# Seven-product pairs of a gated MLP: order of the products, buffers and loads of the weight sums

## Chip, cores and metric

The kernel runs on one core of a Trainium2 chip. The metric is device time in microseconds (us) of one execution, as the median of several runs. The engines are TensorE (PE in the profile, PEld for its weight loads), VectorE (DVE), ScalarE (ACT), GpSimd (POOL) and SyncE (SP, whose queue issues most loads).

## The reference

One decoder layer on 512 tokens of width 1024, in float32. What matters here is its second half, the gated MLP behind the first LayerNorm, with `D_FF` = 2816:

```python
a, u = jnp.split(h @ w_ffn_in[l], 2, axis=-1)
a = causal_dwconv(a, conv_w[l], conv_b[l])        # width 3, along the tokens
f = (jax.nn.gelu(a, approximate=False) * u) @ w_ffn_out[l]
h = layer_norm(ALPHA * h + f, ln2_g[l], ln2_b[l])
```

Ahead of it lie an input projection, block-sparse attention, a pooling branch, two branch projections with gates, an output projection and the first LayerNorm.

## The kernel before

All matrices are float32, and TensorE multiplies them as three products of rounded halves. `split` (L65) makes the halves: ScalarE copies the source into a `hi` tile of the rounded type (L69), and VectorE writes `lo = src - hi` (L70). `mm3` (L182) then issues hi x hi, hi x lo and lo x hi into one accumulator (L184, L185, L186). TensorE's work stands almost without a gap, and everything else is laid out beside it.

Weights come as chunks of 128 x 1024, in the order of a list (`chunks`, L80 to L94). `weights(i)` (L177) makes sure that chunks up to `i + LEAD` (3 ahead) have been fetched; `fetch` (L98) loads a chunk into a `wraw` buffer (three of them) by SP's queue and splits it into a `whi` and a `wlo` buffer from a ring of five (`RING`).

The input projection of the MLP has 22 pairs `f`, each with 128 columns of `a` and 128 of `u`. Pairs 0 to 3 and 18 to 21 are multiplied plainly, 512 tokens at a time. Pairs 4 to 17 (`SEVEN`) use a scheme with seven half-size products in the place of eight: the 2 x 2 blocks are the two halves of the inner dimension (`k1`, `k2`), the two halves of the tokens (`t1`, `t2`), and the weights of `a` and `u`. For it, sums of weights are needed. A pair's four chunks are

- A: the weights of `a`;
- X: the `u` weights' second half added to both halves of `a` (in a rearranged order), made by two DMAs into an `xraw` buffer, a load by SP (L131) and an accumulating one by GpSimd's queue (L132);
- D: the second half of `u`'s weights alone;
- Y: a sum made by VectorE from A and X in two steps (L144).

`fetch_sums` (L126) starts X's two DMAs up to `AHEAD` (5) chunks ahead; `fetch_seven` (L135) loads A and D when their chunk is fetched, forms Y, and splits all four. A, D and Y take `wraw` buffers.

`seven(f)` (L693) does the products of a pair, each of 12 matmuls of 256 columns (`s_mm`, L684), in three PSUM banks: `ba` (its right half is `chain`, in the profile `sa`), `bb` (`low`, `sb`) and `bc` (`c11`, `sc`). Written order: A's first half into `chain` (called A0 below); a ScalarE copy of `chain` into `y` (L699); X0 into `low`; a copy of `low` into `u` (L701); then the left-over product of the pair before (`pending`, Y1 into that pair's `chain`, followed by its `gated`); Y0 onto `chain`; a copy of it into `u` (L705); A1 into `c11`; D0 onto `low`; VectorE adds `low` to `u` (L708); X1 onto `chain`; VectorE adds `chain` to `u` (L710) and writes `y + c11` into the left half of `ba` (L711). Y1 is left for the next pair. `gated` (L621) applies the convolution, gelu and the product with `u`, and writes the pair's slice of `fT`.

The order in the program is a priority, not the order of execution: the instructions of each engine are put into a fixed sequence when the kernel is built, and one may be placed ahead of another that was written earlier if its inputs are planned to be ready sooner. On the chip each engine follows its sequence. Behind the stage the output projection runs on `fT` with sums of its own, and then the second LayerNorm.

Of the kernel before, what the change touches and what calls it, by code (L numbers as in the profile page):

```python
# [8 lines left out]
F32 = mybir.dt.float32  # L9
F32R = mybir.dt.float32r  # L10
AF = mybir.ActivationFunctionType
ALU = mybir.AluOpType
PSUM = bass.MemoryType.PSUM

P = 128
S = 512
D = 1024
# [20 lines left out]
KH = NF // 2  # L38
TAIL = 8
SEVEN = tuple(range(4, 18))  # L40
AHEAD = 5
PRODUCTS = ("T3", "B11", "B21", "T1", "T2", "B22", "T4")


# [1 line left out]
def layer_kernel(ctx: ExitStack, tc: tile.TileContext, xT, x, w_v, w_c, rel_bias, invcnt, w_group,  # L46
                 pscale, w_br, w_out, lnr, w_fi, convp, w_fo, out):
    nc = tc.nc
    const = ctx.enter_context(tc.tile_pool(name="const", bufs=1))
    wp = ctx.enter_context(tc.tile_pool(name="wp", bufs=1))  # L50
# [7 lines left out]
    def bank(name):  # L58
        return ps.tile([P, S], F32, tag="ps", name=name)
# [5 lines left out]
    def split(hi, lo, src, copy=None):  # L65
        if copy:
            copy(hi, src)
        else:
            nc.scalar.activation(hi, src, AF.Copy)  # L69
        nc.vector.tensor_tensor(lo, src, hi.bitcast(F32), op=ALU.subtract)  # L70
# [17 lines left out]
    fi_at = {}  # L88
# [9 lines left out]
    def fetch(pool=None, early=None):  # L98
        i = state["next"]
        state["next"] = i + 1  # L100
        while sums and xu and fi_at[sums[0], "X"] <= i + AHEAD:
            fetch_sums(sums.pop(0))
        if isinstance(chunks[i], tuple):
            ready[i] = (fetch_fo if i >= FO0 else fetch_seven)(i, *chunks[i])
            return
        raw = wp.tile([P, D], F32, tag="wraw", name=f"wraw{i}", bufs=3)
        if pool is None:
            hi = wp.tile([P, D], F32R, tag="whi", name=f"whi{i}", bufs=RING)
            lo = wp.tile([P, D], F32R, tag="wlo", name=f"wlo{i}", bufs=RING)
        else:  # L110
            hi = pool.tile([P, D], F32R, name=f"whi{i}")
            lo = pool.tile([P, D], F32R, name=f"wlo{i}")
        parts = 2 if early else 1
        for c in range(parts):
            sl = slice(c * (D // parts), (c + 1) * (D // parts))
            (nc.scalar if early else nc.sync).dma_start(raw[:, sl], chunks[i][:, sl])
            split(hi[:, sl], lo[:, sl], raw[:, sl], fast if early and c == 0 else None)
            if c == 0 and early:
                early()
        ready[i] = (hi, lo)  # L120

    raws = {}
    sums = list(SEVEN)
    xu = None

    def fetch_sums(f):  # L126
        x_ = raws[f, "X"] = xu.tile([P, D], F32, tag="xraw", name=f"xraw{f}", bufs=2)
        a, u = w_fi[2 * f], w_fi[2 * f + 1]
        v = x_.rearrange("p (a c) -> p a c", a=2)
        (pst, pn), (est, _) = u.ap  # L130
        nc.sync.dma_start(v, bass.AP(tensor=u.tensor, offset=u.offset, ap=[[pst, pn], [0, 2], [est, S]]))  # L131
        nc.gpsimd.dma_start(v, bass.AP(tensor=a.tensor, offset=a.offset,  # L132
                                       ap=[[pst, pn], [u.offset + S - a.offset, 2], [est, S]]), accum_op=ALU.add)

    def fetch_seven(i, f, q):  # L135
        n = S if q == "D" else D
        if q == "X":
            raw = raws[f, "X"]
        else:
            raw = raws[f, q] = wp.tile([P, D], F32, tag="wraw", name=f"wraw{i}", bufs=3)[:, :n]  # L140
        if q == "Y":
            a, x_ = raws[f, "A"], raws[f, "X"]
            for c, o in ((slice(0, S), x_[:, S:]), (slice(S, D), raw[:, :S])):
                nc.vector.tensor_tensor(raw[:, c], o, a[:, c], op=ALU.add)  # L144
        elif q != "X":
            nc.sync.dma_start(raw, w_fi[2 * f] if q == "A" else w_fi[2 * f + 1][:, S:])
        hi = wp.tile([P, D], F32R, tag="whi", name=f"whi{i}", bufs=RING)[:, :n]
        lo = wp.tile([P, D], F32R, tag="wlo", name=f"wlo{i}", bufs=RING)[:, :n]
        split(hi, lo, raw)
        return hi, lo  # L150
# [4 lines left out]
    def piece(c):  # L155
        return slice(c * D, min((c + 1) * D, KH * S))
# [20 lines left out]
    def weights(i):  # L177
        while state["next"] <= min(i + LEAD, state["limit"]):
            fetch()
        return ready[i]  # L180

    def mm3(out_, w, a, start, stop, **kw):  # L182
        (wh, wl), (ah, al) = w, a
        nc.tensor.matmul(out_, wh, ah, start=start, stop=False, **kw)  # L184
        nc.tensor.matmul(out_, wh, al, start=False, stop=False, **kw)  # L185
        nc.tensor.matmul(out_, wl, ah, start=False, stop=stop, **kw)  # L186

    def split3(v, a):
        return tuple(t.rearrange("p (a c) -> p a c", a=a) for t in v)
# [30 lines left out]
    for kt in range(KT):  # L220
        xr = aw.tile([P, S], F32, tag="tmp", name=f"xr{kt}", bufs=TMP)
        if kt == 0:
            load_x(kt, xr, slice(0, 256), nc.vector.tensor_copy)
            fetch(early=lambda: load_x(kt, xr, slice(256, 512), nc.vector.tensor_copy))
        else:
            load_x(kt, xr)
            if kt % 2 == 0:
                fetch()
# [271 lines left out]
    ytiles = [ypool.tile([P, S], F32, name=f"y{j}") for j in range(2)]  # L500
# [120 lines left out]
    def gated(j, a, u, sign=None):  # L621
        y = ytiles[j % 2]
        nc.scalar.activation(y, a, AF.Identity, bias=cvp[:, j, 3:4], scale=cvp[:, j, 2:3])
        nc.vector.scalar_tensor_tensor(y[:, 1:], a[:, :S - 1], cvp[:, j, 1:2], y[:, 1:], op0=ALU.mult, op1=ALU.add)  # L624
        nc.vector.scalar_tensor_tensor(y[:, 2:], a[:, :S - 2], cvp[:, j, 0:1], y[:, 2:], op0=ALU.mult, op1=ALU.add)
        nc.scalar.activation(y, y, AF.Gelu)
        if sign:
            nc.vector.scalar_tensor_tensor(fT[:, j, :], y, sign, u, op0=ALU.mult, op1=ALU.mult)
        else:
            nc.vector.tensor_tensor(fT[:, j, :], y, u, op=ALU.mult)  # L630
# [12 lines left out]
    fT = fw.tile([P, NF, S], F32, name="fT")  # L643
# [7 lines left out]
    t1, t2 = slice(0, 256), slice(256, 512)  # L651
    k1, k2 = slice(0, 4), slice(4, 8)
# [26 lines left out]
    for n in ("nT1", "T3", "nT2", "T4"):  # L679
        t_form(n)  # L680
    state["limit"] = len(chunks) - 1
    pending = []

    def s_mm(f, q, part, act_, b, start, skip=True):  # L684
        wh, wl = split3(weights(fi_at[f, q]), 4 if q == "D" else KT)
        for k in range(4):
            mm3(b, (wh[:, 4 * part + k, :], wl[:, 4 * part + k, :]), (act_[0][:, k, :], act_[1][:, k, :]),
                start and k == 0, k == 3, skip_group_check=not start)

    def whole(k, t):  # L690
        return hT_hi[:, k, t], hT_lo[:, k, t]

    def seven(f):  # L693
        ba, bb, bc = (bank(f"s{q}{f}") for q in "abc")
        chain, low, c11 = ba[:, 256:], bb[:, :256], bc[:, :256]
        y = ytiles[f % 2]
        u = xu.tile([P, S], F32, tag="u", name=f"u{f}", bufs=2)
        s_mm(f, "A", 0, whole(k1, t1), chain, True)
        nc.scalar.activation(y[:, t1], chain, AF.Copy)  # L699
        s_mm(f, "X", 0, tt["T3"], low, True)  # L700
        nc.scalar.activation(u[:, t2], low, AF.Copy)  # L701
        if pending:
            pending.pop()()
        s_mm(f, "Y", 0, tt["nT2"], chain, False)
        nc.scalar.activation(u[:, t1], chain, AF.Copy)  # L705
        s_mm(f, "A", 1, whole(k2, t1), c11, True)
        s_mm(f, "D", 0, tt["T4"], low, False)
        nc.vector.tensor_tensor(u[:, t1], u[:, t1], low, op=ALU.add)  # L708
        s_mm(f, "X", 1, tt["nT1"], chain, False)
        nc.vector.tensor_tensor(u[:, t2], u[:, t2], chain, op=ALU.add)  # L710
        nc.vector.tensor_tensor(ba[:, t1], y[:, t1], c11, op=ALU.add)  # L711

        def close():
            s_mm(f, "Y", 1, whole(k2, t2), chain, False)
            gated(f, ba, u, -1.0)

        pending.append(close)
# [3 lines left out]
    xu = xus.enter_context(tc.tile_pool(name="xu", bufs=1, reuse_waits="tile"))  # L721
    last = max(SEVEN)
    for f in range(RING // 2, last + 1):
        if f in SEVEN:
            seven(f)
            continue
        for j in range(max(RING, 2 * f), 2 * f + 2):
            hb[j] = bank(f"fi{j}")
            fi_mm(j, hb[j], slice(0, S))
            if pending:  # L730
                pending.pop()()
        gated(f, hb[2 * f], hb[2 * f + 1])

    spread = []
    for f in range(last + 1, NF):
        for j in range(2 * f, 2 * f + 2):
# [13 lines left out]
            elif pieces:  # L750
                c = piece(pieces.pop(0))
# [3 lines left out]
        if early:  # L755
            c = early.pop(0)
# [176 lines left out]
```

## Time and profile before

| | |
|---|---|
| median of 3 runs | 651.52 us (651.47 to 652.38) |
| profiled execution | 649.74 us, of which the span is 648.0 us |
| granted TensorE clock, mean | 0.996 |
| TensorE busy | 635.7 us (98% of the span) |
| VectorE, ScalarE, GpSimd busy | 449.5, 328.0, 111.6 us |
| matmuls `sa` of the seven-product pairs | first at 348.0, last at 499.4 us |

Busy shares are means over the whole span, and matmuls overlap each other, so a busy TensorE is not one at its peak. Whether TensorE lost time is read from the starts of its matmuls: in an undisturbed stretch those of 256 columns start 0.12 us apart. A row of the timeline has the start, the duration, the engine, the line, the operation and its tiles, and in brackets the idle time before it with what ended it.

### The profile page before, as it was taken

The numbers are of one execution on the slowest core, as the hardware profiler recorded it, in microseconds if no ns is written. First come the engines' busy times: TensorE is split into PE (matmuls) and PEld (weight loads), VectorE is DVE, ScalarE is ACT, GpSimd is POOL, SyncE is SP. The second block draws the span as 40 slices with busy tenths as digits, with TensorE's granted clock in tenths as the row PEclk, the third lists the DMA queues.
The fourth block names the chain that finished last, engine by engine and source line by source line (L and its number), as shares of the span: only waits on it lengthen the run. The fifth ranks groups of instructions, "written<-read, shape, count | busy, mean of one in ns | idle before, by whom it ended". The sixth has DMA issues, their size and how long they took to land.

```text
span 648.0 us, 9322 instructions
## 1 busy us (share of the span) xinstructions
PE 635.7 (98%) x3586; PEld 551.4 (85%) x3586; DVE 449.5 (69%) x666; ACT 328.0 (51%) x475; POOL 111.6 (17%) x153
## 2 busy tenths in 40 slices
PE   9999999999999999999999999999999999999994
PEld 6888787877888888888999999998998888888884
DVE  6466665564532576299667888787986859698596
ACT  6547556675522333215444556455665337465452
POOL 1605361211000123300010101010100201123302
PEclk9999999999999999999999999999999999999998
DMA  9643222212222227404056686677635895989905
GB/s 323 197 166 99 82 81 82 74 67 89 74 95 98 91 98 286 136 1 162 2 150 173 170 208 155 179 179 188 165 128 163 274 264 137 218 188 193 282 4 129
DMA packets 32540, 94.79 MB, mean 146 GB/s; under 512 B 3688, under 2 KB 3944, under 8 KB 32240
## 3 DMA queue, kind: packets, MB, share of 16 engines
q1 hardware_dynamic: 22832, 66.91, 30.4%
q0 software_dynamic: 9088, 26.24, 20.7%
q10 hardware_dynamic: 576, 1.05, 0.5%
q8 instruction: 28, 0.46, 0.3%
q14 instruction: 16, 0.13, 0.1%
HBM read 91.02 MB, written 3.17 MB: 145 GB/s over the span
## 4 chain that ended last, share of the span: by engine, by line
PE 91%; DVE 3%; POOL 2%; DMA 1%; ACT 1%; issue 1%; DVEq 0%; ACTq 0%; POOLq 0%
PE fi L186 5%; PE fi L184 5%; PE fi L185 5%; PE g L184 5%; PE g L186 4%; PE g L185 4%; PE sa L184 4%; PE sa L186 4%; PE sa L185 4%; PE v L285 3%; PE wo L186 2%; PE br L186 2%; PE br L184 2%; PE wo L184 2%; PE wo L185 2%; PE br L185 2%
## 5 line engine op out<-in xcount | busy, mean ns | idle before, releaser
L70 DVE TENSOR_TENSOR wlo<-wraw,whi 128x1024 fp32r<-128x1024 f32 (+1 forms) x119 | 144.1, 1214 | 59.2 <-ACT whi L69 57.7
L69 ACT ACTIVATE whi<-wraw 128x1024 fp32r<-128x1024 f32 (+1 forms) x118 | 117.2, 996 | 131.9 <-PE g L185 23.6
L186 PE MATMUL fi<-hT_hi,wlo 128*128 128x512 f32 (+1 forms) x168 | 56.7, 339 | 0.0
L185 PE MATMUL fi<-hT_lo,whi 128*128 128x512 f32 (+1 forms) x168 | 56.7, 339 | 0.0
L184 PE MATMUL fi<-hT_hi,whi 128*128 128x512 f32 (+1 forms) x168 | 56.4, 340 | 0.0
L184 PE MATMUL g<-xT_hi,whi 128*128 128x512 f32 x128 | 50.3, 393 | 0.0
L186 PE MATMUL g<-xT_hi,wlo 128*128 128x512 f32 x128 | 49.9, 390 | 0.0
L185 PE MATMUL g<-xT_lo,whi 128*128 128x512 f32 x128 | 49.8, 389 | 0.0
L132 POOL DMA_DIRECT2D xraw<-in_w_fi x14 | 17.0, 1215 | 183.7 <-DVE y L624 70.2
L69 ACT ACTIVATE whi<-tw 128x1024 fp32r<-128x1024 f32 (+1 forms) x30 | 29.4, 982 | 21.6 <-DMA tw<-in_w_fo 8.1
L70 DVE TENSOR_TENSOR wlo<-tw,whi 128x1024 fp32r<-128x1024 f32 (+1 forms) x30 | 33.3, 1127 | 8.4 <-ACT whi L69 8.4
L185 PEld LDWEIGHTS fi<-hT_lo,whi 128*128 128x128 f32 x168 | 31.9, 190 | 3.5
L186 PEld LDWEIGHTS fi<-hT_hi,wlo 128*128 128x128 f32 x168 | 31.9, 190 | 3.3
L184 PEld LDWEIGHTS fi<-hT_hi,whi 128*128 128x128 f32 x168 | 31.6, 190 | 3.3
L184 PE MATMUL sa<-hT_hi,whi 128*128 128x256 f32 x112 | 31.9, 285 | 2.0 <-ACT whi L69 1.9
L186 PE MATMUL sa<-hT_hi,wlo 128*128 128x256 f32 x112 | 31.7, 284 | 0.0
L185 PE MATMUL sa<-hT_lo,whi 128*128 128x256 f32 x112 | 31.6, 283 | 0.0
L184 PE MATMUL sb<-T_hi,whi 128*128 128x256 f32 x112 | 31.5, 282 | 0.0
L184 PE MATMUL sa<-nT_hi,whi 128*128 128x256 f32 x112 | 31.5, 281 | 0.0
L186 PE MATMUL sa<-nT_hi,wlo 128*128 128x256 f32 x112 | 31.3, 279 | 0.0
L185 PE MATMUL sa<-nT_lo,whi 128*128 128x256 f32 x112 | 31.3, 279 | 0.0
L185 PE MATMUL sb<-T_lo,whi 128*128 128x256 f32 x112 | 31.3, 279 | 0.0
(250 smaller groups left out, 1762.8 us busy)
## 6 DMA issues: line engine op xcount, KB each, us to landing
wraw<-in_w_fi SPq DMA_DIRECT2D x30, 512.0 KB, 3.6
wraw<-in_w_c SPq DMA_DIRECT2D x28, 512.0 KB, 3.4
tw<-in_w_fo POOLq DMA_DIRECT2D x20, 512.0 KB, 8.3
xraw<-in_w_fi SPq DMA_DIRECT2D x14, 512.0 KB, 4.9
xraw<-in_w_fi POOLq DMA_DIRECT2D x14, 512.0 KB, 5.7
wraw<-in_w_fo SPq DMA_DIRECT2D x10, 512.0 KB, 5.1
tw<-in_w_fo SPq DMA_DIRECT2D x10, 512.0 KB, 6.6
wraw<-in_w_br SPq DMA_DIRECT2D x8, 512.0 KB, 3.3
```

The source lines that it names most:

```text
L69: nc.scalar.activation(hi, src, AF.Copy)
L70: nc.vector.tensor_tensor(lo, src, hi.bitcast(F32), op=ALU.subtract)
L132: nc.gpsimd.dma_start(v, bass.AP(tensor=a.tensor, offset=a.offset, ap=[[pst, pn], [u.offset + S - a.offset, 2], [est, S]]), accum_op=ALU.add)
L184: nc.tensor.matmul(out_, wh, ah, start=start, stop=False, **kw)
L185: nc.tensor.matmul(out_, wh, al, start=False, stop=False, **kw)
L186: nc.tensor.matmul(out_, wl, ah, start=False, stop=stop, **kw)
L285: nc.tensor.matmul(bs[j], xs_[j][a], (wh, wl)[b], start=kt == 0 and n == 0, stop=False)
```

## The change

It touches only the seven-product pairs.

- `fetch_sums` becomes `fetch_raw`, which starts the loads of A, X and D, each with a distance of its own: 4, 5 and 6 chunks ahead. The three kinds stand in the order A, X, D on SP's queue.
- A keeps the tag `wraw` with its three buffers; D gets two quarter-size buffers of its own (`draw`, 128 x 512).
- Y is written over A in A's buffer and takes none of its own.
- In `seven`, A's second product follows its first, and the left-over product of the pair before comes third: A0, A1, Y1 of the pair before, X0, Y0, D0, X1.
- The copy of A0 goes to a small tile of its own (`p1`, 128 x 256, two buffers) in the place of `ytiles`; the sums `u` are kept in the pair's slice of `fT`, where the result goes, and the tile `u` is gone.

```diff
-AHEAD = 5
+AHEAD = {"A": 4, "X": 5, "D": 6}
...
     def fetch(pool=None, early=None):
...
-        while sums and xu and fi_at[sums[0], "X"] <= i + AHEAD:
-            fetch_sums(sums.pop(0))
+        for q, ahead in AHEAD.items():
+            while coming[q] and (xu or q == "A") and fi_at[coming[q][0], q] <= i + (ahead if xu else 0):
+                fetch_raw(coming[q].pop(0), q)
...
-    sums = list(SEVEN)
+    pending = []
+    coming = {q: list(SEVEN) for q in "DAX"}
     xu = None

-    def fetch_sums(f):
-        x_ = raws[f, "X"] = xu.tile([P, D], F32, tag="xraw", name=f"xraw{f}", bufs=2)
+    def fetch_raw(f, q):
         a, u = w_fi[2 * f], w_fi[2 * f + 1]
-        v = x_.rearrange("p (a c) -> p a c", a=2)
-        (pst, pn), (est, _) = u.ap
-        nc.sync.dma_start(v, bass.AP(tensor=u.tensor, offset=u.offset, ap=[[pst, pn], [0, 2], [est, S]]))
-        nc.gpsimd.dma_start(v, bass.AP(tensor=a.tensor, offset=a.offset,
-                                       ap=[[pst, pn], [u.offset + S - a.offset, 2], [est, S]]), accum_op=ALU.add)
+        if q == "A":
+            r = wp.tile([P, D], F32, tag="wraw", name=f"araw{f}", bufs=3)
+            nc.sync.dma_start(r, a)
+        elif q == "D":
+            r = xu.tile([P, S], F32, tag="draw", name=f"draw{f}", bufs=2)
+            nc.sync.dma_start(r, u[:, S:])
+        else:
+            r = xu.tile([P, D], F32, tag="xraw", name=f"xraw{f}", bufs=2)
+            v = r.rearrange("p (a c) -> p a c", a=2)
+            (pst, pn), (est, _) = u.ap
+            nc.sync.dma_start(v, bass.AP(tensor=u.tensor, offset=u.offset, ap=[[pst, pn], [0, 2], [est, S]]))
+            nc.gpsimd.dma_start(v, bass.AP(tensor=a.tensor, offset=a.offset,
+                                           ap=[[pst, pn], [u.offset + S - a.offset, 2], [est, S]]),
+                                accum_op=ALU.add)
+        raws[f, q] = r

     def fetch_seven(i, f, q):
         n = S if q == "D" else D
-        if q == "X":
-            raw = raws[f, "X"]
-        else:
-            raw = raws[f, q] = wp.tile([P, D], F32, tag="wraw", name=f"wraw{i}", bufs=3)[:, :n]
+        raw = raws[f, "A" if q == "Y" else q]
         if q == "Y":
-            a, x_ = raws[f, "A"], raws[f, "X"]
-            for c, o in ((slice(0, S), x_[:, S:]), (slice(S, D), raw[:, :S])):
-                nc.vector.tensor_tensor(raw[:, c], o, a[:, c], op=ALU.add)
-        elif q != "X":
-            nc.sync.dma_start(raw, w_fi[2 * f] if q == "A" else w_fi[2 * f + 1][:, S:])
+            for c, o in ((slice(0, S), raws[f, "X"][:, S:]), (slice(S, D), raw[:, :S])):
+                nc.vector.tensor_tensor(raw[:, c], o, raw[:, c], op=ALU.add)
...
     def seven(f):
...
-        y = ytiles[f % 2]
-        u = xu.tile([P, S], F32, tag="u", name=f"u{f}", bufs=2)
+        y = xu.tile([P, 256], F32, tag="p1", name=f"p1f{f}", bufs=2)
+        u = fT[:, f, :]
         s_mm(f, "A", 0, whole(k1, t1), chain, True)
-        nc.scalar.activation(y[:, t1], chain, AF.Copy)
+        nc.scalar.activation(y, chain, AF.Copy)
+        s_mm(f, "A", 1, whole(k2, t1), c11, True)
+        if pending:
+            pending.pop()()
         s_mm(f, "X", 0, tt["T3"], low, True)
         nc.scalar.activation(u[:, t2], low, AF.Copy)
-        if pending:
-            pending.pop()()
         s_mm(f, "Y", 0, tt["nT2"], chain, False)
         nc.scalar.activation(u[:, t1], chain, AF.Copy)
-        s_mm(f, "A", 1, whole(k2, t1), c11, True)
         s_mm(f, "D", 0, tt["T4"], low, False)
         nc.vector.tensor_tensor(u[:, t1], u[:, t1], low, op=ALU.add)
         s_mm(f, "X", 1, tt["nT1"], chain, False)
         nc.vector.tensor_tensor(u[:, t2], u[:, t2], chain, op=ALU.add)
-        nc.vector.tensor_tensor(ba[:, t1], y[:, t1], c11, op=ALU.add)
+        nc.vector.tensor_tensor(ba[:, t1], y, c11, op=ALU.add)
```

More of the change, by code (lines that the diff above doesn't have):

```diff
@@ L681, in layer_kernel @@
     state["limit"] = len(chunks) - 1
-    pending = []
     def s_mm(f, q, part, act_, b, start, skip=True):
```

## The prediction

> **What bounds the kernel now.** I read the page first, then the waits of TensorE, then a table of windows over the stage that the change touches, then TensorE's own timeline wherever that table showed fewer matmuls. The page, the busy line and the shares of the chain that ended last:
>
> ```profile
> span 648.0 us, 9322 instructions
> PE 635.7 (98%) x3586; PEld 551.4 (85%) x3586; DVE 449.5 (69%) x666; ACT 328.0 (51%) x475; POOL 111.6 (17%) x153
> PE 91%; DVE 3%; POOL 2%; DMA 1%; ACT 1%; issue 1%; DVEq 0%; ACTq 0%; POOLq 0%
> ```
>
> TensorE is the bound. The change takes no matmul away, so it can only give back time in which TensorE waits in the seven-product stage. Next come the windows there: busy time and count of PE, PEld, DVE, ACT and POOL, then the granted clock and the DMA share. Below them stand the only waits of TensorE longer than half a microsecond in all between 337 and 490 us (total, times, longest).
>
> ```profile
> 357.00:367.00 10.00, 10.00 (x87) 10.00 (x86) 8.25 (x11) 5.86 (x9) 1.21 (x1) 1.00 0.72 184
> 397.00:407.00 10.00, 10.00 (x84) 9.85 (x84) 8.64 (x12) 6.01 (x9) 1.20 (x1) 1.00 0.62 140
> 407.00:417.00 10.00, 9.15 (x77) 8.95 (x76) 6.21 (x11) 4.13 (x7) 1.20 (x1) 1.00 0.79 228
> 427.00:437.00 10.00, 10.00 (x87) 9.97 (x86) 7.97 (x13) 5.60 (x9) 1.20 (x1) 1.00 0.78 205
> 437.00:447.00 10.00, 8.81 (x71) 8.37 (x70) 7.27 (x12) 5.37 (x7) 1.20 (x1) 1.00 0.71 180
> 467.00:477.00 10.00, 10.00 (x87) 10.00 (x86) 9.41 (x14) 5.79 (x10) 0.00 (x0) 1.00 0.45 119
> PE sa L184 <- ACT whi L69: 1.9, 2, 1.1
> PEld sa L184 <- ACT whi L69: 2.3, 2, 1.3
> ```
>
> A full window holds 86 or 87 matmuls of 256 columns at clock 1.00. Three windows hold 84, 77 and 71. The timeline of TensorE at those places gives the loss:
>
> ```profile
> 400.60 0.28 PE L186 MATMUL sc<-hT_hi,wlo 128*128 128x256 f32 x1
> 400.77 0.39 PE L184 MATMUL sa<-nT_hi,whi 128*128 128x256 f32 x1
> 401.00 0.28 PE L185 MATMUL sa<-nT_lo,whi 128*128 128x256 f32 x1
> 401.12 0.39 PE L184 MATMUL sb<-T_hi,whi 128*128 128x256 f32 x1
> 401.34 0.28 PE L185 MATMUL sb<-T_lo,whi 128*128 128x256 f32 x1
> 410.84 0.28 PE L186 MATMUL sb<-T_hi,wlo 128*128 128x256 f32 x1
> 411.97 0.39 PE L184 MATMUL sa<-hT_hi,whi 128*128 128x256 f32 x1 [0.85 <-ACT whi L69]
> 412.19 0.28 PE L185 MATMUL sa<-hT_lo,whi 128*128 128x256 f32 x1
> 441.98 0.28 PE L186 MATMUL sc<-hT_hi,wlo 128*128 128x256 f32 x1
> 443.34 0.39 PE L184 MATMUL sa<-hT_hi,whi 128*128 128x256 f32 x1 [1.08 <-ACT whi L69]
> 443.56 0.28 PE L185 MATMUL sa<-hT_lo,whi 128*128 128x256 f32 x1
> 443.95 0.39 PE L184 MATMUL sa<-hT_hi,whi 128*128 128x256 f32 x1
> 444.17 0.28 PE L185 MATMUL sa<-hT_lo,whi 128*128 128x256 f32 x1
> ```
>
> In a row without a gap (401.00 to 401.12) one matmul starts 0.12 us after the other. So the excess is (411.97 - 410.84 - 0.12) + (412.19 - 411.97 - 0.12) = 1.01 + 0.10 = 1.11 us at the first big stall. At the second it is 1.24 + 0.10 + 0.27 + 0.10 = 1.71 us. The two short ones near 401 give 0.05 + 0.11 + 0.10 = about 0.25 us. All of it is **3.1 us**, 0.47% of the time: that is the most the change can win, and the clock cannot add to it. A difference of 0.2%, 1.3 us of 651.52, is about what a measurement of this kernel can tell from no change.
>
> What ended the two big stalls:
>
> ```profile
> 406.03 8.79 SPq L146 DMA_DIRECT2D wraw<-in_w_fi  x3
> 410.86 1.06 ACT L69 ACTIVATE whi<-wraw 128x1024 fp32r<-128x1024 f32 x1 [0.78 <-DMA wraw<-in_w_fi]
> SPq L146 <- DVE wlo L70: 43.5, 13, 6.3
> SPq L146 <- DVE wraw L144: 27.8, 6, 7.5
> 432.72 1.06 ACT L69 ACTIVATE whi<-wraw 128x1024 fp32r<-128x1024 f32 x1 [1.27 <-DMA wraw<-in_w_fi]
> 439.35 0.63 ACT L69 ACTIVATE whi<-wraw 128x512 fp32r<-128x512 f32 x1 [3.88 <-PE sa L185]
> 442.23 1.06 ACT L69 ACTIVATE whi<-wraw 128x1024 fp32r<-128x1024 f32 x1 [0.40 <-PE sc L185]
> ```
>
> The first is a late load. SP issues it at 406.03, when a `wraw` buffer comes free; it lands 4.8 us later, ACT copies it in 1.06 us (410.86 to 411.92), and the matmul starts at 411.97. SP's queue waited 43.5 us for VectorE's splits and 27.8 us for the Y sums (L144) before such loads. The second ends a longer chain: at 432.72 ACT again waited for a load of `wraw`; then its queue stood for 3.88 us in front of the D split until a matmul gave back a ring slot of `whi`; the A split, further back in that queue, ended at 443.29, and TensorE started at 443.34.
>
> **The change part by part.** *Loads.* A, D and Y shared three `wraw` buffers, so A of the next pair waited until the Y sum of this pair had read its A, or the D split had ended. Now Y is written over A, A has all three buffers and is issued a pair ahead, and D has two of its own. Bytes and DMA count stay. What is added is order on SP: for each pair A, the u half of X, then D, so D stands behind X's wait for `xraw` and X behind A's wait. Each issue is one short instruction on SP, and the loads have about a pair (84 matmuls by 0.12 = 10.1 us) against the 4.8 us of the landing above. I put the late load at 0: the first stall, 1.11 us, goes. If that cover failed, the same 1.11 us would come back in each pair that it fails in.
>
> *Ring slots.* A's slot was held until A's second product, the fifth of seven; now it is released after the second. X, which takes that slot, was needed second and is now needed fourth. One product is 12 matmuls, 1.4 us; so the distance from release to need grows from three products (4.3 us) to eight (11.4 us). D's slot still comes from X of the pair before, so the 3.88 us wait can recur; but D's own use stays sixth, and the A behind it no longer starts from a late load. I put the second stall, 1.71 us, at 0 as well; between 0 and 1.71 this is the less certain term.
>
> *The sum in place* is the same two VectorE operations. *The copy of A0* goes to a tile of its own, so it no longer waits for the gated product; no TensorE wait above names it, so 0. *u in `fT`* changes an address only.
>
> *The copies of the accumulators* are where it can lose. ACT copies `low` after X0, and D0 may then add to `low`; ACT copies `chain` after Y0, and X1 may then add to it. Written order before: three products between X0 and D0, two between Y0 and X1. After: one each. The profile shows one such turn at its tightest (last matmul of X0, the copy, first of D0 at 401.12, shown above), and the groups:
>
> ```profile
> 400.37 0.28 PE L186 MATMUL sb<-T_hi,wlo 128*128 128x256 f32 x1
> 400.69 0.38 ACT L701 ACTIVATE u<-sb 128x256 f32<-128x256 f32 x1
> L69 ACT ACTIVATE whi<-xraw 128x1024 fp32r<-128x1024 f32 x14 | 14.9, 1062 | 14.3 <-DMA xraw<-in_w_fi 6.5 <-PE sa L185 5.7 <-PE sb L185 1.9
> L705 ACT ACTIVATE u<-sa 128x256 f32<-128x256 f32 x14 | 5.4, 385 | 7.0 <-PE sa L186 7.0
> ```
>
> The copy ends at 401.07 and TensorE goes on at 401.12: from the last matmul's start to the next on that bank it takes 401.12 - 400.37 = 0.75 us when ACT is free. One product between gives 0.12 + 1.43 = 1.55 us, so 0.8 us is spare. ACT works in order; a full split that has just begun holds it for 1.06 us and would cost 1.06 - 0.8 = 0.26 us; two in a row would cost 1.3 us; a free ACT costs nothing. That is 0 to 1.3 us at each of 28 turns. A gain is excluded here, as the distance only shrinks. ACT is busy 5.9 us in 10, and the losses at copies that before shows are the 0.05 to 0.11 us near 401, although D0 follows on X0 within 0.75 us there. So I take the low end: about 0.02 us a turn, 0.5 us in all, estimated from one turn in fifteen at 0.26 us.
>
> The Trainium skill, page "PSUM — Partial Sum Buffer", section "PSUM bank collisions raise a hardware error", says that no two engines may touch one bank at once and that one guards by bank, not by address. By that rule the turns cannot be shortened, which speaks against the new order, and the trace agrees, with 401.07 to 401.12. It also names VectorE's write beside the chain, which no wait above half a microsecond here shows.
>
> **Sum.** -1.11 - 1.71 + 0.5 = -2.3 us; the quarter microsecond near 401 is of the copies' kind and stays. The profiled execution took 649.74 us, 1.74 around its span of 648.0; it becomes 647.4. The median of the runs shown, 651.52, lies 1.78 above it, so I forecast 651.52 - 2.3 = **649.2 us**. Its own range is 648.4 (all 3.1 us gone, no new wait) to 650.2.
>
> **The rivals.** *One, a new wait at the copies, slower.* Splits are ready earlier because loads are, so the order on ACT puts them in front of the copies, and in each pair one turn pays. It decides from (2.8 + 1.3) / 14 = 0.3 us a pair: a copy held by 1.1 us of ACT work. At 0.45 us a pair it is 14 x 0.45 - 2.8 = +3.5, **655.0 us**; at break-even it is 652.8. For it: ACT's 1.06 us splits and the spare of 0.8 us. Against it: full windows at 357 and 467 with ACT at the same load. Chance 0.28.
>
> *Two, the ring or VectorE stays the bound, no change.* `whi` still has five slots, and VectorE is busy 8.0 to 9.4 us of 10 in full windows. Then only the late load's 1.11 us go, the D split still stands in front of A, and with the copies' 0.5 us the time is 651.52 - 1.1 + 0.5 = **650.9 us**. For it is the 3.88 us wait, which names a matmul and not a load. Chance 0.16.
>
> *Three, the written order is not the run order.* In before, these came within half a microsecond:
>
> ```profile
> 395.00 0.29 PE L184 MATMUL sa<-hT_hi,whi 128*128 128x256 f32 x1
> 395.25 0.28 PE L184 MATMUL sb<-T_hi,whi 128*128 128x256 f32 x1
> 395.49 0.29 PE L184 MATMUL sc<-hT_hi,whi 128*128 128x256 f32 x1
> ```
>
> The three products A0, X0 and A1 are opened together, so the order is set at build time by readiness and the new row of products may hardly show. Then loads alone act and new holes can open elsewhere as easily as old ones close: about **651 us**. Chance 0.06.
>
> **How the numbers follow.** Forecast 0.50, rival one 0.28, two 0.16, three 0.06. Faster by over 0.2% is the forecast alone: 0.50. Within 0.2% are two and three: 0.22. Slower is rival one: 0.28. The range goes from 648.1 (3.1 us gone and 0.3 us of spread between runs) up to 654.0, into the middle of rival one; about 0.05 is left out below and 0.13 above.
>
> **What would show it.** Right: windows of ten microseconds in this stage all with 86 or 87 matmuls, no TensorE wait for ACT's `whi`, SP's A loads issued some ten microseconds before their split, and loads' waits on VectorE gone. Wrong: TensorE waits that name the copies of `low` or `chain` (ACT `u`), several per pair, would be rival one; a wait for `whi` behind a D split would be rival two; A0, X0 and A1 still opened together would be rival three. A stall behind the stage, in the last projection, would be outside every step here.

## The result and the profile after

The changed kernel takes **646.68 us** (median of 4 runs, 646.13 to 647.37) against 651.5 us before (651.27 to 652.38): a ratio of 0.9924, 95% interval 0.9907 to 0.9941. Timed again it took 646.45 against 650.87 us, 0.9925 (0.9904 to 0.9947). The forecast was 649.2 us, with a range of 648.1 to 654.0: right in its sign, half of the size, and the range was missed by 1.4 us. The profiled execution took 647.0 us.

The windows of the stage after the change, with the same columns as before:

```profile
span 645.3 us, 9324 instructions
357.00:367.00 10.00, 10.00 (x87) 10.00 (x86) 8.30 (x12) 5.77 (x8) 1.22 (x1) 1.00 0.61 149
397.00:407.00 10.00, 10.00 (x87) 10.00 (x86) 9.53 (x14) 6.23 (x10) 1.20 (x1) 1.00 0.67 171
407.00:417.00 10.00, 10.00 (x87) 10.00 (x87) 7.70 (x12) 5.46 (x8) 1.20 (x1) 1.00 0.86 208
437.00:447.00 10.00, 10.00 (x87) 10.00 (x86) 8.87 (x13) 6.60 (x10) 1.20 (x1) 1.00 0.71 186
```

The windows that held 84, 77 and 71 matmuls all hold 87, and between 337 and 500 us no wait of TensorE is named at all. What is left are waits of queues that hold nothing up. Of SP's queue the three longest, and two of ScalarE's (total, times, longest):

```profile
SPq L140 <- DVE wlo L70: 58.1, 12, 7.6
SPq L132 <- DVE wlo L70: 18.7, 7, 3.7
SPq L135 <- DVE wlo L70: 14.6, 7, 4.0
ACT whi L69 <- PE sa L191: 17.4, 24, 2.5
ACT fT L708 <- PE sb L192: 5.8, 14, 0.5
```

L132, L140 and L135 are the loads of A, X and D. Loads still wait for their buffers, 91 us in these three rows, where the prediction expected such waits to be gone, but they are early enough: no ScalarE split of A, D or Y waits for its load any more (before, two did, for 0.78 and 1.27 us). The length of the stage is read from one group of its matmuls, before (first row) and after:

```profile
L184 PE MATMUL sa<-hT_hi,whi x112: 277/283/387, 348.0 to 499.2; 128*128 128x256 f32 x112
L190 PE MATMUL sa<-hT_hi,whi x112: 277/283/290, 349.0 to 496.7; 128*128 128x256 f32 x112
```

From first to last start it is 151.2 us before and 147.7 after: **3.5 us shorter**. The slowest of them also fell from 387 to 290 ns. The stage began 1.0 us later in this execution of the changed kernel, and behind it 148.6 us follow in the place of 148.8. These last 0.2 us are no gain of their own: after the change one more matmul of the plain pairs (0.23 us) stands ahead of the last one of this group. Counted up to the last matmul of the plain pairs, from 348.0 to 534.2 us before and from 349.0 to 531.5 after, the gain is 3.7 us.

### The profile page after: what moved, and what is told of

The parts are those of the page before. It is cut to its first block, busy times and chain, and to the rows that moved or that the text cites. A ratio compares the mean times of both kernels' runs of the same rounds, so it can differ in the third digit from the quotient of the medians.

```text
span 645.3 us, 9324 instructions
## 1 busy us (share of the span) xinstructions
PE 634.8 (98%) x3586; PEld 551.2 (85%) x3586; DVE 449.4 (70%) x666; ACT 328.7 (51%) x475; POOL 110.9 (17%) x153
## 4 chain that ended last, share of the span: by engine, by line
PE 94%; DVE 2%; POOL 2%; ACT 1%; DMA 0%; issue 0%; DVEq 0%; ACTq 0%; POOLq 0%
PE fi L190 5%; PE fi L192 5%; PE fi L191 5%; PE g L190 5%; PE g L191 5%; PE g L192 5%; PE sa L190 4%; PE sa L192 4%; PE sa L191 4%; PE v L291 3%; PE wo L192 2%; PE br L192 2%; PE br L190 2%; PE wo L190 2%; PE wo L191 2%; PE br L191 2%
## 5 line engine op out<-in xcount | busy, mean ns | idle before, releaser
L70 DVE TENSOR_TENSOR wlo<-wraw,whi 128x1024 fp32r<-128x1024 f32 (+1 forms) x77 | 100.4, 1308 | 50.8 <-ACT whi L69 49.8
L69 ACT ACTIVATE whi<-wraw 128x1024 fp32r<-128x1024 f32 (+1 forms) x76 | 78.8, 1040 | 97.9 <-PE g L191 23.6
L70 DVE TENSOR_TENSOR wlo<-araw,whi 128x1024 fp32r<-128x1024 f32 x28 | 33.9, 1221 | 6.0 <-ACT whi L69 5.7
L69 ACT ACTIVATE whi<-araw 128x1024 fp32r<-128x1024 f32 x28 | 29.4, 1061 | 13.3 <-PE sa L191 6.1
```

## The experiments

**The kernel before, profiled again.** No edit.

> The kernel before, unchanged, profiled a second time. Its first profiled execution (649.74 us) was 1.8 us shorter than the median of its other runs. Theory S (stage): the executions differ inside the seven-product stage, because waits for loads there vary; then this profile shows more than the 3.1 us of gaps between TensorE's matmuls in that stage, near 4 to 5 us, with the first matmul of the stage at 348 us again. Theory B (begin): they differ ahead of the first projection, where loads of the first weights land; then the stage has its 3.1 us again and its first matmul starts at 349 us or later. Ratio to before 1.000.

Measured: ratio 0.9994 (0.9984 to 1.0004), median 650.65 us (649.87 to 652.37); the profiled execution took 650.11 us. The two big stalls stand at the same two places, with the same excess to 0.02 us:

```profile
412.38 0.39 PE L184 MATMUL sa<-hT_hi,whi 128*128 128x256 f32 x1 [0.84 <-ACT whi L69]
443.71 0.39 PE L184 MATMUL sa<-hT_hi,whi 128*128 128x256 f32 x1 [1.08 <-ACT whi L69]
```

So the stalls are no chance of one execution. The stage has its 3.1 us of gaps again, which speaks for theory B, but it began at 348.4 us, 0.4 later than in the first profile, where theory B asked for 349 or later. What makes the longer runs longer is not shown (below).

**The loads and buffers alone.** The changed `fetch`, `fetch_raw` and `fetch_seven`, with `seven` as before:

```diff
-        y = xu.tile([P, 256], F32, tag="p1", name=f"p1f{f}", bufs=2)
-        u = fT[:, f, :]
+        y = ytiles[f % 2]
+        u = xu.tile([P, S], F32, tag="u", name=f"u{f}", bufs=2)
...   # products in the order of before
```

> Only the loads and buffers of the change: A in three buffers a pair ahead, D in two of its own, Y over A; products in the old order, copies and sums in the old tiles. If late loads are what the change cures (theory L), this alone gives most of it: 0.992 to 0.994, no gap left in the stage. If the order of the products is needed to free ring slots (theory R), the loads give only the first stall, 1.1 us: 0.998, and a wait for whi behind a D split stays.

Measured: 0.9943 (0.9928 to 0.9958), and no gap in the stage.

**The order of the products alone.** In the kernel before:

```diff
         nc.scalar.activation(y[:, t1], chain, AF.Copy)
+        s_mm(f, "A", 1, whole(k2, t1), c11, True)
+        if pending:
+            pending.pop()()
         s_mm(f, "X", 0, tt["T3"], low, True)
         nc.scalar.activation(u[:, t2], low, AF.Copy)
-        if pending:
-            pending.pop()()
         s_mm(f, "Y", 0, tt["nT2"], chain, False)
         nc.scalar.activation(u[:, t1], chain, AF.Copy)
-        s_mm(f, "A", 1, whole(k2, t1), c11, True)
```

> Only the order of the products: A0, A1, Y1 of the pair before, X0, Y0, D0, X1; loads, buffers, copies as before. Theory L: loads stay late, so 0.998 to 1.004, with gaps that end with ScalarE's whi after a load of wraw. Theory R: the ring slots come free earlier and about half of the gain is there: 0.995 to 0.997. The prediction's fear, copies with only one product between, would show as gaps ended by ScalarE's u, over 3 us in all: above 1.004.

Measured: 0.9946 (0.9929 to 0.9963), no gap either, and no wait of TensorE that names a copy. The windows where the stalls were, first for the loads alone, then for the order alone:

```profile
407.00:417.00 10.00, 10.00 (x87) 10.00 (x86) 9.00 (x14) 5.81 (x9) 1.20 (x1) 1.00 0.71 182
437.00:447.00 10.00, 10.00 (x87) 10.00 (x86) 8.61 (x13) 5.81 (x9) 1.20 (x1) 1.00 0.80 199
```

```profile
407.00:417.00 10.00, 10.00 (x86) 10.00 (x86) 9.25 (x13) 6.61 (x11) 1.20 (x1) 1.00 0.70 174
437.00:447.00 10.00, 10.00 (x87) 10.00 (x86) 8.88 (x14) 6.07 (x10) 1.20 (x1) 1.00 0.78 220
```

Each half of the change closes both stalls by itself. That neither theory L nor theory R foresees: with the order alone the loads come much as before (the two that were issued at 406.0 and 406.6 us are issued at 404.9 and 407.9), and SP's waits for buffers are longer (59.1 us for L144, where before had 27.8):

```profile
SPq L146 <- DVE wraw L144: 59.1, 12, 6.4
SPq L146 <- DVE wlo L70: 34.0, 13, 5.3
```

**The places of the copies alone.**

```diff
-        y = ytiles[f % 2]
-        u = xu.tile([P, S], F32, tag="u", name=f"u{f}", bufs=2)
+        y = xu.tile([P, 256], F32, tag="p1", name=f"p1f{f}", bufs=2)
+        u = fT[:, f, :]
```

> Only the places of the copies: A0's copy in a tile of its own, u in the pair's slice of fT; loads and order as before. No gap of before is ended by either, so both theories expect 0.999 to 1.001; a change of the fixed order of the engines that comes with it could move the two stalls by 1 us either way.

Measured: 0.9966 (0.9952 to 0.998), outside what both expected. One stall of 0.9 us is left near 411 us, the one at 443 is gone, and a new one stands in the last projection (619 us):

```profile
PE sa L184 <- ACT whi L69: 0.7, 1, 0.7
PE fod L185 <- DVE wlo L70: 0.4, 1, 0.4
```

An edit that removes no wait moved both stalls. That points to the fixed sequence of the instructions, which every edit makes anew. It is set out here by products, read from the timelines of TensorE, for the kernel before and for that of the next experiment (the number of matmuls in brackets; `A0.11` is A0 of pair 11). First the place where the two part:

```
before:    X1.8(12) X0.9(10) A1.9(2) Y0.9(2) D9(12) Y1.8(12) A0.10(2) Y0.9(10) X0.10(2)
side held: X1.8(12) X0.9(10) A1.9(2) Y1.8(12) Y0.9(2) D9(12) Y0.9(10) A0.10(2) X0.10(2)
```

Then the places of the first and the second stall, each ahead of an A0:

```
before:    X1.9(12) X0.10(10) A0.11(2) Y0.10(12) D10(10) Y1.9(12) D10(2)
side held: X1.9(12) X0.10(10) A1.10(2) Y1.9(12) Y0.10(2) D10(12) Y0.10(10) A0.11(2)
before:    X0.13(10) A1.13(2) A0.14(2) Y1.12(12) A0.14(10)
side held: X0.13(10) A1.13(2) Y1.12(12) Y0.13(2) D13(12) Y0.13(10) A0.14(2)
```

At both stalls the sequence of before opens A0 some 36 matmuls, 4.3 us, earlier than the regular one does. The matmul waits there for its split, and at the first stall the split for its load. What stands at the parting is on VectorE, in the trace of before:

```profile
399.51 0.42 DVE L710 TENSOR_TENSOR u<-u,sa 128x256 f32<-128x256 f32 x1 [0.60 <-PE sa L186]
399.85 1.22 DVE L757 TENSOR_TENSOR ra<-fT 128x1024 f32<-128x1024 f32 x1
400.98 0.42 DVE L711 TENSOR_TENSOR sa<-y,sc 128x256 f32<-128x256 f32 x1
```

L757 prepares the last projection and has nothing to do with pair 8. It stands between two operations of pair 8 that are written ahead of Y1.8 and work on its bank (that such a product waits for L711 shows once in this trace, with 0.3 us), and just there Y1.8 falls back behind Y0.9 and D9, by 14 matmuls. That the planned end of L711 is what moved it is inferred: no run records the plan.

**That operation held behind the stage.** The edit holds both L757 operations of the stage, that of 351.4 us and that of 399.8. In the kernel before, with `state["last"]` the last VectorE operation of pair 17's `gated`:

```diff
-            nc.vector.tensor_tensor(rd(c), side(0, c, t1), side(0, c, t2), op=ALU.subtract)
+            with tc.issue_after(state["last"].ins):
+                nc.vector.tensor_tensor(rd(c), side(0, c, t1), side(0, c, t2), op=ALU.subtract)
```

> The kernel before with one thing changed: VectorE's differences for the last projection (L757), two of which run inside the stage (at 351 and 400 us), are held behind the gated product of the last seven-product pair. Theory P: the two stalls come from that 1.2 us operation, which falls into pair 11 and throws the fixed sequence of the products out of its period (Y1 of the pair before comes a whole pair late afterwards); then the period holds to the end, no gap is left in the stage although loads, buffers and order are as before, and the ratio is 0.9945 to 0.996. Theory L: late loads and short buffers are the cause by themselves; then gaps of 1 to 3 us stay and the ratio is 0.998 to 1.002.

Measured: 0.9941 (0.9918 to 0.9963), median 647.45 us. The sequence of the matmuls is that of before up to 400.6 us, so the first L757 did not matter to it; from there it keeps its period to the end. The stage has no gap, and the only long wait of TensorE behind 337 us is new and lies in the last projection, where the held operation now comes late:

```profile
407.00:417.00 10.00, 10.00 (x87) 10.00 (x86) 8.60 (x13) 5.93 (x9) 1.20 (x1) 1.00 0.68 179
437.00:447.00 10.00, 10.00 (x86) 10.00 (x85) 8.60 (x13) 5.93 (x9) 1.20 (x1) 1.00 0.72 193
SPq L146 <- DVE wraw L144: 56.6, 10, 7.5
618.42 0.50 PE L185 MATMUL fod<-wlo,sd_hi 128*128 128x512 f32 x1 [0.68 <-DVE wlo L70]
```

What changed at the first stall shows in the last split ahead of A0 of pair 11, and in the first matmul of this A0 (the kernel before had 410.86 and 411.97 us):

```profile
410.88 1.05 ACT L69 ACTIVATE whi<-wraw 128x1024 fp32r<-128x1024 f32 x1
414.89 0.29 PE L184 MATMUL sa<-hT_hi,whi 128*128 128x256 f32 x1
```

The split ends at 411.93 us in this run and at 411.92 in the kernel before. But TensorE comes to A0 at 414.89 us, where the kernel before stood ready for it at 410.96. The two loads of this place moved less, from 406.0 and 406.6 us to 404.2 and 406.5.

Theory P is shown for the kernel before, if not by the pair that the expectation named (the sequence breaks at pair 8, not 11): with its three buffers and its written order of products TensorE is fed without a gap as long as the sequence is regular. The operation is not enough by itself, however: with the loads alone or the order alone it runs inside the stage too (at 402.3 and 399.3 us), and no stall follows. With the order alone the sequence does part from its period there, and finds back to it without a stall.

**The change without the new places of the copies.**

```diff
-        y = xu.tile([P, 256], F32, tag="p1", name=f"p1f{f}", bufs=2)
-        u = fT[:, f, :]
+        y = ytiles[f % 2]
+        u = xu.tile([P, S], F32, tag="u", name=f"u{f}", bufs=2)
...   # loads and products as changed
```

> The change without the new places of the copies: loads, buffers, sum in place and product order as changed, but A0's copy in the gated tile and u in a tile of its own. Its fixed sequence is irregular from pair 10 on, as that of before is, but with loads a pair ahead. Theory P (an irregular sequence stalls): gaps of 1 to 2 us, 0.996 to 0.998. Theory L (only late loads stall): no gap, 0.994 to 0.995.

Measured: 0.996 (0.9943 to 0.9977). Two of the three parts together do worse by their middle than either alone, though the intervals overlap: the sequence is irregular, and no wait for an A0 is named, but 1.2 us are lost when it passes into the plain pairs, in front of a `fi` product that the sequence put among the last seven-product ones:

```profile
480.60 0.28 PE L192 MATMUL sa<-nT_hi,wlo 128*128 128x256 f32 x1
480.79 1.06 ACT L69 ACTIVATE whi<-wraw 128x1024 fp32r<-128x1024 f32 x1 [1.01 <-PE sa L191]
481.90 0.50 PE L190 MATMUL fi<-hT_hi,whi 128*128 128x512 f32 x1 [1.03 <-ACT whi L69]
```

The load of this chunk had landed at 464.5 us. Its split waited for a matmul to give back a ring slot. So early loads by themselves don't make an irregular sequence safe: the ring can hold it up too.

**The changed kernel with the operation held as well.** The edit of the side operation on the changed kernel.

> The changed kernel with L757's differences held behind the stage as well. The changed kernel has no gap left in the stage, so both theories expect the same time as the changed kernel, 0.9935 to 0.995; an operation moved behind the stage could cost up to 2 us there if VectorE is late for the last projection.

Measured: 0.9934 (0.9913 to 0.9955), 647.32 us; no gap in the stage. It is not better than the changed kernel, and no version here was.

**The changed kernel again.**

> The changed kernel, unchanged, timed again with more runs. The profiles of before and after differ by 3.55 us inside the seven-product stage and by 0.2 us behind it; the begin of the kernel varies by about 1 us from execution to execution. If that is all (theory S), the ratio is 0.9942 (3.75 of 650.9), between 0.993 and 0.9955. If the first result, 0.9924, was no chance (theory X, a gain outside the stage), it is 0.992 to 0.993 again.

Measured: 0.9925 (0.9904 to 0.9947), 646.45 us (645.96 to 647.87), its profiled execution 646.38 us. By its middle theory X; the interval holds both.

**More profiles of both kernels.** No edits.

> The kernel before, unchanged, one more profile, to find where its longer executions lose their time: both profiles so far (649.7 and 650.1 us) lie at the short end of its runs (649.6 to 653.4 us), and 3.75 us of the gain are seen in profiles where the medians differ by 4.4. Theory S: gaps in the stage grow (over 3.1 us, at other places too). Theory B: the stage keeps 3.1 us of gaps, and the time to the first matmul of the stage varies, 347.8 to 349.5 us, or the tail does.

> As the run before it: one more profile of the unchanged kernel before. Theory S: over 3.1 us of gaps in the stage whenever the time is over 651 us. Theory B: 3.1 us of gaps whatever the time is.

> As the run before it: one more profile of the unchanged kernel before. Theory S: over 3.1 us of gaps in the stage whenever the time is over 651 us. Theory B: 3.1 us of gaps whatever the time is.

> The changed kernel, unchanged, a third profile. Both theories: no gap in the stage, stage length 147.9 us (first to last of its matmuls), whatever the begin does; a gap here would say that its loads too are late in some executions.

Measured: before 649.83, 650.6 and 649.73 us; after 646.41 us. The same group as above, for the three profiles of before and then the one of after:

```profile
L184 PE MATMUL sa<-hT_hi,whi x112: 277/283/387, 348.1 to 499.2; 128*128 128x256 f32 x112
L184 PE MATMUL sa<-hT_hi,whi x112: 277/283/388, 348.9 to 500.0; 128*128 128x256 f32 x112
L184 PE MATMUL sa<-hT_hi,whi x112: 277/283/388, 348.0 to 499.2; 128*128 128x256 f32 x112
L190 PE MATMUL sa<-hT_hi,whi x112: 277/283/290, 347.9 to 495.6; 128*128 128x256 f32 x112
```

The stage takes 151.1 or 151.2 us in all profiles of before and 147.7 in that of after. What varies among profiles is the begin, 348.0 to 348.9 us: theory B for these. No profile caught one of the executions above 651 us (a further execution of before on the same occasion took 652.53 us), so what is longer in those is not shown.

## Why the prediction was right or wrong

**The bound and the place: right.** TensorE bounds the kernel, the gaps in its matmuls were most of what there was to win in the stage, those that the prediction added up came to 3.0 to 3.1 us in all five profiles of before, and the change closed every one of them.

**The step that failed most: the offset of the median.** The prediction worked out 647.4 us for a profiled execution and then added the 1.78 us by which the median of before lay above its profiled execution, as though that belonged to any kernel. The changed kernel's profiled executions took 647.0, 646.38 and 646.41 us: within 0.35 us of its medians, 646.68 and 646.45. Of the miss of 2.5 us (649.2 against 646.68) 2.1 are this step, and of the 2.75 us in the second comparison 1.7. That 647.0 lies so near the 647.4 that was worked out is luck in part: in that execution the stage began 1.0 us later, and the other two profiles lie at 646.4. Before has longer executions that were not seen of the changed kernel: in the second comparison its 15 runs went from 649.56 to 653.42 us, a spread of 3.9, the 6 of after from 645.96 to 647.87, 1.9. The fastest runs there differ by 3.6 us, about as the profiles do; the medians by 4.4. Why the runs of before spread further, and why all five of its profiled executions (649.73 to 650.6 us) lie below its medians (650.65 to 651.52), stays open: no profile fell on a long execution.

**Terms that were mis-sized.** The copies were put at +0.5 us, and nothing was lost there; the 0.25 us of short gaps near 401 were to stay and went. The prediction counted on one product between X0 and D0 because so they are written. The fixed sequence puts more there: in the changed kernel, pair 11 runs

```
X0.11(12) Y0.11(11) Y1.10(12) Y0.11(1) D11(12)
```

with 24 matmuls between X0 and D0, not 12. In the changed kernel no gap of TensorE is ended by a copy. The Trainium skill's rule to guard PSUM by bank and not by address (page "PSUM — Partial Sum Buffer", section "PSUM bank collisions raise a hardware error") thus had no price there; no run here tests the rule itself. And the gain is 3.7 us, not 3.1 at most: the gaps of before come to 3.2 to 3.3 us when some of up to 0.11 us that the prediction did not count are added, and the other 0.4 to 0.5 us are a slightly faster pace of the matmuls in all three profiles of after. In these, 182.5 us lie between the first matmul of the stage and the last of the plain pairs. With the loads alone, the order alone or the held operation in either kernel it is 183.0 or 183.1 us, though gaps come to 0.1 us there at most. The cause of this pace stays open. So the profiled gain is 3.7 us, where the prediction had 2.3.

**The mechanism: half right.** The first stall is a late load and the second a late split, as the prediction read them. The step on the ring misread which slot was held. It gave A's slot to the next X. But the row at 442.23 us that the prediction shows, `0.40 <-PE sc L185`, is the split of A of pair 14 waiting for the last matmuls of A1 of pair 13, and A0.14 stands right behind these in the sequence: its split of 1.06 us had to fall into the gap. And late loads and held slots did not make the stalls by themselves: with the two L757 operations held behind the stage both stalls are gone, though the lines for loads, buffers and products are those of before. The prediction showed products opened together near 395 us and made of that its rival three, with a chance of 0.06, in which the change would hardly act. In fact the sequence was the point, and the change acted all the same: the sequence is set at build time, and an irregular one asked for A0 some 4.3 us too early at both stalls. Each part of the change gave a new sequence, and the loads slack for an irregular one; which of the two keeps the changed kernel itself free of gaps was not separated.

**The rivals.** One (copies, slower) did not occur in any of the kernels. Two (the ring stays the bound) did not occur in the changed kernel, and the held operation shows that five slots are enough for a regular sequence; the change without the new places of the copies shows that an irregular one can still wait for a slot.

## What to carry to other kernels

Where instructions are ordered when the kernel is built, look for what broke the period before looking for a scarce buffer: write the sequence of the products down for a regular pair and for the stalled one, and see which foreign operation stands where they part. A gap ceiling from one profiled execution holds for the gaps of that execution alone; forecast profile against profile, and compare the fastest runs too, as an offset between a profile and a median need not be inherited by a changed kernel.

## What had not been expected

Small edits that remove no wait moved the time by 0.3% (the places of the copies alone, 0.9966), and two parts of the change together did no better than one (0.996 against 0.9943 and 0.9946): here the sequence that came out mattered more than the sum of the parts. The begin of the kernel varied by 1.0 us among executions of both kernels (first matmul of this group at 347.9 to 349.0 us), more than a quarter of the effect that was being measured.
